# Moving two of a weight pair's four loads from GpSimd's queue to SyncE's

## The chip, the cores and the metric

The kernel runs on one core of a Trainium2 chip. A core has five engines that run side by side and meet through semaphores: PE (TensorE, matrix products), VectorE (DVE in the profile), ScalarE (ACT), GpSimd (POOL) and SyncE (SP). The engines that issue DMAs put them into queues; 16 DMA engines carry the bytes. The metric is the device time of one execution in microseconds. Before the change it was 1569.61 us in the median of 3 runs (1569.16 to 1570.11).

## The reference

Two layers over 512 tokens of width 1024, in fp32. Each layer normalizes x, projects it, runs three token mixers beside each other (windowed attention, a short convolution, a state space model), merges them by gates, and adds the result. Then comes the part that this change touches, the gated feed-forward:

```python
x = x + merged @ w_mix_o[i]
h = rmsnorm(x, norm_ffn[i])
gt, up = jnp.split(h @ w_ffn_in[i], 2, axis=-1)     # 1024 x (2 x 2816)
x = x + (jax.nn.silu(gt) * up) @ w_ffn_out[i]       # 2816 x 1024
```

## The kernel before, in words

Activations lie transposed, channels on the 128 partitions and 512 tokens along them. All weights stream in from DRAM. A product of fp32 matrices is made of three products of parts: a weight tile is split into a rounded high part (a cast on ScalarE) and the remainder (a subtraction on VectorE, line 190, in `lo_of`), and PE multiplies high by high, high by low and low by high (`mm3`, line 270).

The weights are a list of items, in the order of their use. A **plain item** is one load of a tile `raw` (line 185, issued by SyncE), one cast (line 205) and one subtraction. A **pair item** serves most of the feed-forward: of each layer's 22 tiles of hidden channels, tiles 6 to 21 (16 items) and the output products of three groups of tiles (6 items), 22 items a layer and 44 in all. There, two weight matrices and two halves of the operand are multiplied as a 2 x 2 block product with seven products in the place of eight (`seven_products`). For it the weight blocks a11, a12, a21, a22 and four sums of them are wanted. A pair item needs four DMAs from `wsp`, each reading rows of a pre-arranged stretch [a11 a12 | a21 a11 | a22 a21]:

- r2 (line 175, 512 KB) loads a21 and a11; a second DMA (line 176, 512 KB) adds a22 and a21 onto it in flight, so that r2 holds the sums a21 + a22 and a11 + a21;
- r1 (line 177, 512 KB) loads a11 and a12, with nothing added onto it;
- r4 (line 178, 256 KB) loads a22, with nothing added onto it.

From them VectorE makes r3, two further sums of r2 and r1 (lines 216 and 218), ScalarE the high parts h1 to h4 (lines 214, 221, 225, 229), and VectorE the remainders l1 to l4 (line 190). In the profile's groups these names lose their numbers: r1 to r4 are all `r`, h1 to h4 `h`, l1 to l4 `l`.

r1, r2 and r3 come from one pool of five buffers, r4 from a large pool that many temporaries share. A load waits until the earlier user of its buffer is done. Items are fetched two ahead of the one being split, and split until PE has some 48 units of work ready (`feed`).

The sums of the feed-forward's output that go through seven products are added onto `xkept` in DRAM by DMAs with accumulation (lines 1176 and 1179, 256 KB each, issued by GpSimd), eight per group and 24 per layer. `xkept` begins with eight plain stores of the residual (line 1256, SyncE), and it is read back at the end of the layer (line 1233, SyncE). In `seven_products`, ScalarE copies the partial sum pb out (line 1143, `ga`) before PE goes on adding to pb.

Each engine and each issuing queue works in program order, and an instruction that waits holds those behind it. The order on each engine is set when the kernel is built: a scheduler walks the program with modelled times and appends each instruction to its engine's queue. So a load's place in a queue says behind which others it waits.

## Time and profile before

| what | value |
|---|---|
| median of 3 runs | 1569.61 us |
| the profiled execution's own time | 1570.92 us |
| its span, from the first to the last instruction | 1568.9 us |
| PE busy | 1543.0 us (98%) |
| VectorE busy | 1169.3 us (75%) |
| ScalarE busy | 728.8 us (46%) |
| GpSimd busy | 270.5 us (17%) |
| DMA queue 0 (GpSimd's): bytes, share of 16 DMA engines | 100.05 MB, 27.0% |
| DMA queue 1 (SyncE's): bytes, share of 16 DMA engines | 119.60 MB, 23.9% |

Rows of the profile are read so: a time from the span's start, a duration, the engine, the line, the operation, output and input, the count; in brackets how long the engine was idle before it and what ended that idle time. `SPq` is SyncE's queue. A busy PE is not a PE at its peak, since matmuls overlap and their ends are modelled.

### The profile page before, as it was taken

What the parts mean: (1) busy time and instruction counts of PE and PEld (TensorE: products, weight loads), DVE (VectorE), ACT (ScalarE), POOL (GpSimd) and SP (SyncE); (2) the same over time, 40 slices, a digit from 0 to 9 for tenths busy, and PEclk for the clock granted to TensorE, in tenths of its full rate; (3) what the DMA queues carried; (4) which work ended last, traced back from release to release, by engine and by line L of the source; (5) the groups of instructions that cost most, each with busy time, mean ns of one, the idle gap of its engine ahead of it and who ended that gap; (6) DMA issues with size and microseconds to landing.
All of it is one profiled execution on the core that took longest, in us unless ns stands there. A gap on an engine that the chain in (4) does not pass through costs nothing.

```text
span 1568.9 us, 24688 instructions
## 1 busy us (share of the span) xinstructions
PE 1543.0 (98%) x9204; PEld 1350.1 (86%) x9204; DVE 1169.3 (75%) x2292; ACT 728.8 (46%) x1312; POOL 270.5 (17%) x453
## 2 busy tenths in 40 slices
PE   9999999999999999999999999999999999999996
PEld 7777878888888899999888777788888889999996
DVE  7985869765668687978668667897476767878876
ACT  4345543334444365655524554233344434656653
POOL 0301023210000124333021011222100002234221
PEclk9999999999999999999999999999999999999998
DMA  6422334442532679888534232354334237799863
GB/s 225 126 81 79 82 96 131 131 118 79 182 112 95 183 175 221 201 222 195 189 113 130 75 84 87 102 135 131 94 122 167 88 121 197 181 224 212 213 142 118
DMA packets 91959, 221.73 MB, mean 141 GB/s; under 512 B 21600, under 2 KB 27008, under 8 KB 91840
## 3 DMA queue, kind: packets, MB, share of 16 engines
q0 software_dynamic: 36096, 100.05, 27.0%
q1 hardware_dynamic: 55456, 119.60, 23.9%
q8 instruction: 72, 1.18, 0.3%
q10 hardware_dynamic: 288, 0.52, 0.1%
q14 instruction: 47, 0.39, 0.1%
HBM read 193.89 MB, written 22.02 MB: 138 GB/s over the span
## 4 chain that ended last, share of the span: by engine, by line
PE 82%; DVE 6%; DMA 5%; issue 4%; POOL 1%; ACT 1%; DVEq 0%; SPq 0%; POOLq 0%; ACTq 0%
PE pg L270 17%; PE pc L270 11%; PE py L270 8%; PE pd L270 8%; PE pb L270 8%; PE pfo L270 6%; PE px L270 6%; PE pfu L270 4%; PE pfg L270 4%; DMA r<-wsp 3%; PE pu L270 1%; PE pqb L270 1%; PE pz L270 1%; PE pS L852 1%; DVE wlo L190 1%
## 5 line engine op out<-in xcount | busy, mean ns | idle before, releaser
L205 ACT CAST whi<-raw 128x1024 fp32r<-128x1024 f32 (+2 forms) x214 | 195.5, 917 | 431.6 <-PE pg L270 115.3
L190 DVE TENSOR_TENSOR wlo<-raw,whi 128x1024 fp32r<-128x1024 f32 (+2 forms) x214 | 225.9, 1056 | 91.9 <-ACT whi L205 84.1
L190 DVE TENSOR_TENSOR l<-r,h 128x1024 fp32r<-128x1024 f32 (+1 forms) x176 | 187.9, 1086 | 12.1 <-ACT h L225 6.1
L270 PE MATMUL pg<-hi,whi 128*128 128x512 f32 x384 | 152.2, 396 | 0.0
L270 PE MATMUL pg<-hi,wlo 128*128 128x512 f32 x384 | 150.4, 392 | 0.0
L270 PE MATMUL pg<-lo,whi 128*128 128x512 f32 x384 | 150.0, 391 | 0.0
L270 PE MATMUL pd<-lo,h 128*128 128x256 f32 x528 | 148.2, 283 | 0.0
L270 PE MATMUL pd<-hi,l 128*128 128x256 f32 x528 | 147.4, 283 | 0.0
L270 PE MATMUL pd<-hi,h 128*128 128x256 f32 x528 | 147.2, 283 | 0.0
L270 PE MATMUL pb<-hi,h 128*128 128x256 f32 x352 | 100.0, 285 | 3.2 <-ACT ga L1143 2.9
L270 PEld LDWEIGHTS pd<-lo,h 128*128 128x128 f32 x528 | 100.9, 192 | 0.0
L270 PEld LDWEIGHTS pd<-hi,h 128*128 128x128 f32 x528 | 100.5, 192 | 0.0
L270 PEld LDWEIGHTS pd<-hi,l 128*128 128x128 f32 x528 | 100.5, 192 | 0.0
L270 PE MATMUL pb<-lo,h 128*128 128x256 f32 x352 | 99.4, 283 | 0.0
L270 PE MATMUL pb<-hi,l 128*128 128x256 f32 x352 | 98.9, 283 | 0.0
L178 POOL DMA_DIRECT2D r<-wsp x44 | 34.2, 778 | 339.4 <-PE pfu L270 330.6
L270 PEld LDWEIGHTS pg<-hi,whi 128*128 128x128 f32 x384 | 72.1, 188 | 15.8 <-DVE ph_c L354 0.4
L270 PEld LDWEIGHTS pg<-hi,wlo 128*128 128x128 f32 x384 | 72.1, 188 | 15.2
L270 PEld LDWEIGHTS pg<-lo,whi 128*128 128x128 f32 x384 | 72.2, 188 | 14.3
L270 PE MATMUL pc<-hi,whi 128*128 128x512 f32 x192 | 77.3, 402 | 1.7 <-ACT qr L815 1.7
L270 PE MATMUL pc<-lo,whi 128*128 128x512 f32 x192 | 76.0, 396 | 0.0
L270 PE MATMUL pc<-hi,wlo 128*128 128x512 f32 x192 | 75.5, 393 | 0.0
(303 smaller groups left out, 4310.4 us busy)
## 6 DMA issues: line engine op xcount, KB each, us to landing
raw<-wst SPq DMA_DIRECT2D x140, 512.0 KB, 3.5
r<-wsp POOLq DMA_DIRECT2D x132, 512.0 KB, 5.7
raw<-wst SPq DMA_DIRECT2D x56, 256.0 KB, 2.8
r<-wsp POOLq DMA_DIRECT2D x44, 256.0 KB, 5.8
raw<-wst SPq DMA_DIRECT2D x16, 384.0 KB, 3.0
xkept<-ga POOLq DMA_DIRECT2D x24, 256.0 KB, 7.3
xkept<-ub POOLq DMA_DIRECT2D x24, 256.0 KB, 7.7
xkept<-xres SPq DMA_DIRECT2D x16, 256.0 KB, 3.7
```

Source lines behind the costliest of these rows:

```text
L178: nc.gpsimd.dma_start(r4[:, :n], wsp[i, :, 2048 : 2048 + n])
L190: V.tensor_tensor(out=lo, in0=raw, in1=hi.bitcast(F32), op=ALU.subtract)
L205: A.copy(hi[:, c], raw[:, c])
L270: T.matmul(o, a, b, start=start and i == 0, stop=stop and i == 2, skip_group_check=more)
L852: T.matmul(pS[par][:, hp, keys], qt[a][rows, 2 * k + hp], kt[b][rows, k, keys], start=i == 0, stop=i == 2,)
```

## The change

The loads of r1 and r4 are issued by SyncE. r2 and its accumulation stay on GpSimd.

```diff
             n = half[0]
             nc.gpsimd.dma_start(r2[:, : 2 * n], wsp[i, :, 1024 : 1024 + 2 * n])
             nc.gpsimd.dma_start(r2[:, : 2 * n], wsp[i, :, 2048 : 2048 + 2 * n], accum_op=ALU.add)
-            nc.gpsimd.dma_start(r1[:, : 2 * n], wsp[i, :, 0 : 2 * n])
-            nc.gpsimd.dma_start(r4[:, :n], wsp[i, :, 2048 : 2048 + n])
+            nc.sync.dma_start(r1[:, : 2 * n], wsp[i, :, 0 : 2 * n])
+            nc.sync.dma_start(r4[:, :n], wsp[i, :, 2048 : 2048 + n])
             raws.append((i, n, r1, r2, r4))
```

PE, VectorE and ScalarE keep their order. On GpSimd, this is the piece with a group's output sums in layer 0 (the number behind r1, r2, r4, ga and ub is that of the buffer):

```order
 L1176 DMA xkept0_4365<-ga_5848 128x512
 L1179 DMA xkept0_4365<-ub_5849 128x512
 L1176 DMA xkept0_4365<-ga_5929 128x512
 L175 DMA r2_5995<-wsp 128x1024
-L178 DMA r4_6138<-wsp 128x512
 L1179 DMA xkept0_4365<-ub_5930 128x512
-L177 DMA r1_5994<-wsp 128x1024
 L176 DMA r2_5995<-wsp 128x1024
 L1176 DMA xkept0_4365<-ga_5984 128x512
```

The two plain loads between r2 and its accumulation leave; r2 stays behind the three output sums, and the accumulation behind r2.

On SyncE, the first pair item's r1 is placed among the raw loads of the mixers, long before the feed-forward:

```order
 L185 DMA raw_3068<-wst 128x1024
 L185 DMA raw_3089<-wst 128x512
+L177 DMA r1_5020<-wsp 128x1024
 L185 DMA raw_3123<-wst 128x1024
 L185 DMA raw_3150<-wst 128x512
```

A second one (r1_5077) is placed the same way some ten raw loads later, and both again in layer 1.

On SyncE, at the start of the seven-product stretch of layer 0, in the new order:

```order
L185 DMA raw_4961<-wst 128x768
L178 DMA r4_5022<-wsp 128x512
L178 DMA r4_5079<-wsp 128x512
L178 DMA r4_5147<-wsp 128x512
L178 DMA r4_5211<-wsp 128x512
L1256 DMA xkept0_4365<-xres_4068 128x512
L1256 DMA xkept0_4365<-xres_4108 128x512
```

Four r4 loads now stand ahead of the stores to `xkept`. From the last of these stores on, the queue of SyncE holds only r1 and r4 loads up to the next layer's first load (b_c, line 417).

## The prediction

> **What bounds the kernel now.** I read the page first (engine shares, DMA issues), then the windows of the two stretches in which the moved loads are consumed, then who PE and VectorE wait for there, then GpSimd's timeline at one stall.

> ```profile
> span 1568.9 us, 24688 instructions
> PE 1543.0 (98%) x9204; PEld 1350.1 (86%) x9204; DVE 1169.3 (75%) x2292; ACT 728.8 (46%) x1312; POOL 270.5 (17%) x453
> ```

> PE is busy 98% of the span, so a gain can only come out of PE's idle time, and only out of the part that the loads cause. The seven-product stretches run from 536 to 760 us (layer 0) and from 1308 to 1532 us (layer 1):

> ```profile
> core 0: us, PE busy (x) PEld busy (x) DVE busy (x) ACT busy (x) POOL busy (x), PEclk, DMA share, GB/s
> 536.00:760.00 224.00, 221.05 (x1832) 220.18 (x1831) 180.47 (x246) 133.54 (x239) 67.52 (x98) 1.00 0.80 192
> 1308.00:1532.00 224.00, 223.78 (x1861) 223.18 (x1860) 181.22 (x247) 134.72 (x241) 67.60 (x98) 1.00 0.81 194
> 775.00:785.00 10.00, 10.00 (x46) 8.27 (x45) 10.00 (x15) 8.39 (x14) 0.00 (x0) 1.00 0.94 337
> ```

> PE idles 224 - 221.05 = 2.95 us in the first and 0.22 us in the second: together 3.2 us, 0.20% of the time. The granted clock is 1.00 in both. That is the ceiling of any gain here. (The third row gives a price used below: the DMA engines moved 337 GB/s when they were 94% busy.) In layer 0 the idle time has one name:

> ```profile
> PE pb L270 <- ACT ga L1143: 2.9, 2, 1.5
> ```

> Two waits of about 1.5 us, for the copy of pb that frees a partial sum. The copy is late because ScalarE stands behind VectorE, and VectorE behind a load. The one near 692 us:

> ```profile
> 689.66 0.69 DVE L216 TENSOR_TENSOR r<-r,r 128x512 f32<-128x512 f32 x1 [4.33 <-DMA r<-wsp]
> 691.71 0.63 ACT L1164 ACTIVATE ga<-ga 128x512 f32<-128x512 f32 x1 [4.08 <-DVE ga L358]
> 693.18 0.36 ACT L1143 COPY ga<-pb 128x256 f32<-128x256 f32 x1
> ```

> L216 adds r1 to the accumulated r2, so it is r2's accumulation that arrives last. VectorE's waits for that load, first in layer 0's stretch, then in layer 1's:

> ```profile
> DVE r L216 <- DMA r<-wsp: 14.7, 3, 5.6
> DVE r L216 <- DMA r<-wsp: 13.6, 5, 4.9
> ```

> VectorE loses 28.3 us in eight such waits, and PE loses 2.9 us in two: the operands made ahead cover the rest. Layer 1 runs the same program and shows no PE wait, so this cover is just about used up, not plentiful.

> **The change, part by part.** Of an item's four issues, GpSimd keeps r2 (L175) and its accumulation (L176), and loses r1 (L177) and r4 (L178): 44 each, 88 in all.

> *GpSimd's own time.* A quiet item and a crowded one, in the timeline of GpSimd:

> ```profile
> 547.59 0.53 POOL L175 DMA_DIRECT2D r<-wsp  x1 [6.12 <-DVE l L190]
> 549.32 0.53 POOL L177 DMA_DIRECT2D r<-wsp  x1 [1.20 <-DVE l L190]
> 549.84 0.54 POOL L178 DMA_DIRECT2D r<-wsp  x1
> 552.84 0.88 POOL L176 DMA_DIRECT2D r<-wsp  x1 [2.46 <-DMA r<-wsp]
> ...
> 670.36 0.86 POOL L176 DMA_DIRECT2D r<-wsp  x1 [5.31 <-DMA r<-wsp]
> 670.91 1.21 POOL L1176 DMA_DIRECT2D xkept<-ga  x1
> 671.47 1.53 POOL L1179 DMA_DIRECT2D xkept<-ub  x1
> 672.01 1.87 POOL L1176 DMA_DIRECT2D xkept<-ga  x1
> 672.56 1.89 POOL L175 DMA_DIRECT2D r<-wsp  x1
> 673.10 1.90 POOL L178 DMA_DIRECT2D r<-wsp  x1
> 673.65 2.24 POOL L1179 DMA_DIRECT2D xkept<-ub  x1
> 674.22 2.22 POOL L177 DMA_DIRECT2D r<-wsp  x1
> 683.89 0.86 POOL L176 DMA_DIRECT2D r<-wsp  x1 [7.45 <-DMA r<-wsp]
> ```

> An issue holds GpSimd some 0.54 us (549.84 - 549.32 in the quiet item, 673.10 - 672.56 in the crowded one), so 88 x 0.54 = 48 us leave GpSimd. None of it is on the path: in both items r1 and r4 are issued while L176 could not go anyway, because it waits for r2's landing (2.46 us after the last issue in the quiet item, 7.45 us in the crowded one). And in the crowded item r2 itself stands behind the three xkept accumulations, not behind r1 or r4. So L175 and L176 are issued when they are now: 0 us.

> *SyncE's time.* An issue took SyncE 0.33 us (the b_c row below), so 88 x 0.33 = 29 us are added, in stretches where its queue is empty: between 537.5 us, the end of the xkept stores, and b_c at 741.65 us it issues nothing in layer 0. What matters is whether one of these issues waits with weight loads behind it. Rows of SyncE's queue and of GpSimd at the places where the new issues stand among older ones:

> ```profile
> 274.68 7.23 SPq L185 DMA_DIRECT2D raw<-wst  x3
> 275.62 0.57 POOL L177 DMA_DIRECT2D r<-wsp  x1 [13.74 <-DVE apt L358]
> 503.14 1.63 POOL L178 DMA_DIRECT2D r<-wsp  x3 [165.31 <-PE pfu L270]
> 508.09 0.54 POOL L178 DMA_DIRECT2D r<-wsp  x1 [3.32 <-DVE ub L358]
> 516.06 0.33 SPq L1256 DMA_DIRECT2D xkept<-xres  x1
> 524.48 0.54 POOL L175 DMA_DIRECT2D r<-wsp  x1 [15.86 <-DVE l L190]
> 524.90 12.56 SPq L1256 DMA_DIRECT2D xkept<-xres  x4
> 741.65 0.33 SPq L417 DMA_DIRECT2D b_c<-ssb  x1
> ```

> The first r1 stands behind the raw load of 274.68 us; its buffer is free at 275.62 us, under 1 us later, and two more raw loads follow up to 281.9 us. The four r4 loads stand ahead of the store of 516.06 us; the last is free to go at 508.09 us, 8 us before. The 165 us for which GpSimd waited at L178 held nothing back that layer 0 needed: the next r2 went out only at 524.48 us, when VectorE had freed its buffer. I cost the queue on SyncE at 0; if a buffer came later than now, the raw loads behind it would be late by that much.

> *The transfers.* Bytes, shapes and buffers stay. What a load of this kind takes from issue to landing on either queue, on the page:

> ```profile
> raw<-wst SPq DMA_DIRECT2D x140, 512.0 KB, 3.5
> r<-wsp POOLq DMA_DIRECT2D x132, 512.0 KB, 5.7
> raw<-wst SPq DMA_DIRECT2D x56, 256.0 KB, 2.8
> r<-wsp POOLq DMA_DIRECT2D x44, 256.0 KB, 5.8
> ```

> So r1 and r4 may land 2 to 3 us sooner, though these rows mix quiet and crowded stretches. That buys nothing where VectorE waits: there r2's accumulation is last. The question is what r1 and r4 do to r2. Today they follow it in one queue; from SyncE they go beside it, in the crowded items also beside the xkept traffic ahead of it. Bounds on the shift of r2's accumulated landing: if all 512 + 256 KB come in between, 512/337 + 256/337 = 1.5 + 0.8 = +2.3 us. If they are done before, the accumulation no longer finds the rest of r1 on the engines. The rows of L176, its issues and its landing:

> ```profile
> L176 POOL DMA_DIRECT2D r<-wsp x44: 859/878/944, 245.8 to 1502.2; - x44
> DMA to landing us min/median/max: 5.4/5.8/7.7
> ```

> At the stall it took 689.66 - 683.89 = 5.8 us, so at best -0.4 us. Between -0.4 and +2.3 I take +0.4 us, the distance from minimum to median, which is what ordinary sharing costs this transfer today. At the two places without cover that is 2 x 0.4 = +0.8 us on PE; at the other six waits I let the cover swallow it (without cover: 6 x 0.4 = 2.4 us more).

> [...]

> **Sum.** 0 (GpSimd) + 0 (SyncE) + 0.8 (r2 a little later) = +0.8 us on the profiled execution, 1570.92 us, of which 1568.9 us is span. That execution is 1.3 us above the median of the runs, 1569.61 us; on the median the forecast is 1570.4 us. A measurement of this kernel can tell a change from none beyond about 0.2%, 3.1 us: the forecast is no change.

> **Rivals.**

> A. The bursts relax. r1 and r4 out of GpSimd's queue, r2's accumulation comes early enough at both places, and PE's waits go. For it: VectorE's long waits all lie at the xkept bursts, where the queue is fullest. Against it: each burst keeps xkept, r2 and the accumulation, in this order. It needs the accumulation 1.5 us earlier, and the row of L176 allows 0.4. At most all the idle time goes: 1569.6 - 3.2 = 1566.4 us. Chance 0.15.

> B. r2 arrives late, the slower side. r1 goes ahead of or between r2's packets at each burst. For it: 0.80 of the DMA engines' time is taken in the stretch, and r1's wait for its buffer (1.20 us after r2 in the quiet item) puts its issue right into r2's transfer. Against it: total bytes are the same, and part of r1 now goes out while GpSimd still waits. With r1 alone in between, 1.5 us: 2 x 1.5 = 3.0 us at the two stalls, and at the other six, where cover may take half, 6 x 0.75 = 4.5 us: +3.0 to +7.5, 1572.6 to 1577.1 us, middle 1575. It decides from a shift of 0.8 us on (1.6 + 6 x 0.4 = 4.0, or 1.6 with full cover). Chance 0.20. [...]

> C. SyncE's queue is held by an r1 or r4 whose buffer is late, and weight loads stand behind it. The rows above leave about 8 us at 508 us and little at 275 us, with loads made ahead behind it. Losing as much as one wait of the kind of 165 us is excluded, since the same order of issues is kept around it; some 3 us: 1573 us. Chance 0.04.

> **How the numbers follow.** Forecast 0.61, A 0.15, B 0.20, C 0.04. Time 1570.4 us. The range reaches down to A's floor, 1566.4, and up to the middle of B, 1574.8, which leaves out half of B and a little of A, some 0.15. Faster by over 0.2%: A and a trace of the forecast, 0.15, since the ceiling is just that bound; slower: B, C and the forecast's upper edge, 0.26; no change 0.59.

> **What would show it.** GpSimd's busy time falls from 270.5 us by some 50 to 80 us (its issues in a burst last up to 2.2 us). The landing of L177 and L178 falls toward 3 to 4 us. L175 and L176 stay on their places in the bursts; if L176's wait for r2, 7.45 us, grows by 1 us or more, B is at work; if VectorE's eight waits for L216 shrink below 20 us together, A is. PE's idle time in the two windows stays between 2 and 5 us. A gap in SyncE's raw loads after 275 us, or at the same place of layer 1, with PE idle behind it would be C. A gain of more than 3.2 us would prove the ceiling, and so the whole argument, wrong.

## The result, and the profile after

The change made the kernel slower: 1578.86 us in the median of 5 runs (1574.48 to 1583.44), beside 1569.16 us for the kernel before on the same chip. The ratio is 1.0062, with a 95% interval of 1.0045 to 1.0079, or +9.7 us. That lies above the forecast of no change, above the range's end at 1574.8 us, and above all that rival B had been given.

The profiled execution took 1583.44 us, the longest of the five. Its page: span, busy times, and the issues of the moved and the kept loads (count, size, median us from issue to landing).

```profile
span 1581.7 us, 24679 instructions
PE 1548.8 (98%) x9204; PEld 1355.2 (86%) x9204; DVE 1169.9 (74%) x2292; ACT 729.9 (46%) x1312; POOL 222.6 (14%) x365
...
r<-wsp POOLq DMA_DIRECT2D x88, 512.0 KB, 5.8
r<-wsp SPq DMA_DIRECT2D x44, 512.0 KB, 5.1
...
r<-wsp SPq DMA_DIRECT2D x44, 256.0 KB, 5.2
```

GpSimd lost 270.5 - 222.6 = 47.9 us of busy time, just the 48 us of its 88 issues. Nothing came of it. The span is 12.8 us longer. The same windows as before, and the two stretches behind PE's waits in which the granted clock was lower:

```profile
536.00:760.00 224.00, 219.45 (x1801) 218.81 (x1800) 178.49 (x244) 131.42 (x234) 47.57 (x62) 0.98 0.79 190
696.68:703.51 6.83, 5.80 (x27) 5.80 (x28) 6.83 (x13) 4.19 (x9) 1.33 (x2) 0.50 0.96 268
1308.00:1532.00 224.00, 218.87 (x1787) 217.37 (x1786) 177.58 (x243) 130.11 (x232) 48.30 (x63) 0.99 0.81 189
1474.92:1478.33 3.41, 3.41 (x18) 3.41 (x18) 3.41 (x7) 2.02 (x5) 0.00 (x0) 0.50 1.02 287
```

PE idles 4.55 + 5.13 = 9.7 us in the two stretches, where it had idled 3.2 us: 6.5 us more. New is the granted clock, the figure behind the busy times: 0.50 over 6.83 us and over 3.41 us, where it had been 1.00 in the pair stretches. Under the lower clock PE starts a matmul every 0.21 us, in the rest of the pair stretches every 0.12 us. Over the same matmuls of the two stretches PE is busy for 2.28 + 1.56 = 3.8 us longer than before. Together 10.3 of the 12.8 us; about 1 us more is there already at the first pair load (its issue starts at 242.2 us, before at 241.2 us). The five runs lost different amounts of clock: the mean granted clock over the whole run is 0.992 in the profiled one, 0.995 at the median and 0.997 in the fastest (1574.48 us), which is still 5.3 us slower than before. This suggests that the idle time is the steady part of the loss and the clock the varying one; only one of the five runs has a profile to show it.

PE's waits, and VectorE's, in the new profile (sum, times, longest):

```profile
PE pb L270 <- ACT ga L1143: 9.7, 4, 3.1
```

```profile
DVE r L216 <- issue: 41.7, 10, 7.8
```

Both are the chain of the prediction, longer. The profile now puts VectorE's waits down to "issue", but the load is the same one: in the landings of the trace's single DMAs, the accumulation (L176) lands 0.1 us before L216 starts at each of the ten long waits of the pair stretches, and r1 had landed 3 to 10 us earlier. In the profile of before, too, two waits for this load stand under "issue" and are missing from the prediction's eight. They come one item ahead of the bursts of output sums in layer 0:

```profile
615.51 0.69 DVE L216 TENSOR_TENSOR r<-r,r 128x512 f32<-128x512 f32 x1 [1.50 <-issue]
...
678.11 0.69 DVE L216 TENSOR_TENSOR r<-r,r 128x512 f32<-128x512 f32 x1 [3.29 <-issue]
```

So the sum is 33.1 us in ten waits before and 41.7 us in ten after. The largest five waits, in VectorE's timeline, before:

```profile
627.53 0.69 DVE L216 TENSOR_TENSOR r<-r,r 128x512 f32<-128x512 f32 x1 [4.79 <-DMA r<-wsp]
...
739.79 0.69 DVE L216 TENSOR_TENSOR r<-r,r 128x512 f32<-128x512 f32 x1 [5.62 <-DMA r<-wsp]
...
1399.41 0.69 DVE L216 TENSOR_TENSOR r<-r,r 128x512 f32<-128x512 f32 x1 [4.92 <-DMA r<-wsp]
...
1460.08 0.69 DVE L216 TENSOR_TENSOR r<-r,r 128x512 f32<-128x512 f32 x1 [4.78 <-DMA r<-wsp]
```

and the same five places after (the one shown in the prediction, 4.33 us at 689.66, is now the one at 693.77):

```profile
629.94 0.69 DVE L216 TENSOR_TENSOR r<-r,r 128x512 f32<-128x512 f32 x1 [5.88 <-issue]
...
693.77 0.69 DVE L216 TENSOR_TENSOR r<-r,r 128x512 f32<-128x512 f32 x1 [7.33 <-issue]
...
744.26 0.69 DVE L216 TENSOR_TENSOR r<-r,r 128x512 f32<-128x512 f32 x1 [3.44 <-issue]
...
1407.30 0.69 DVE L216 TENSOR_TENSOR r<-r,r 128x512 f32<-128x512 f32 x1 [7.76 <-issue]
...
1470.22 0.69 DVE L216 TENSOR_TENSOR r<-r,r 128x512 f32<-128x512 f32 x1 [7.02 <-issue]
```

Set beside PE's waits for pb behind them, with the wait for the item ahead of each burst (single rows of the timelines, in us; the last row is the sixth long wait of the new profile):

| place | VectorE's wait before | after | the item ahead, before | after | PE's wait before | after |
|---|---|---|---|---|---|---|
| layer 0, first burst of output sums | 4.79 | 5.88 | 1.50 | 1.81 | none | 1.45 |
| layer 0, second burst | 4.33 | 7.33 | 3.29 | 2.01 | 1.39 | 3.10 |
| layer 0, end | 5.62 | 3.44 | | | 1.51 | none |
| layer 1, first burst | 4.92 | 7.76 | 1.36 | 1.01 | none | 2.92 |
| layer 1, second burst | 4.78 | 7.02 | 1.21 | 1.33 | none | 2.18 |
| layer 1, end | 1.34 | 4.14 | | | none | none |

The first five waits grew by 1.09 + 3.00 - 2.18 + 2.84 + 2.24 = 7.0 us, PE's by 6.75 us: in the sum, nearly every microsecond that the load was later reached PE. How much of a wait is covered, that is, does not reach PE, can be worked out from these rows. In layer 1 it is 7.76 - 2.92 = 4.84 and 7.02 - 2.18 = 4.84 us. In layer 0 the item ahead had waited for longer, and what it waited beyond 1.40 us comes on top: 5.88 - 4.84 + (1.81 - 1.40) = 1.45 and 7.33 - 4.84 + (2.01 - 1.40) = 3.10 us, as measured. The same two figures give the wait of before at the second burst, 4.33 - 4.84 + (3.29 - 1.40) = 1.38 us against 1.39 measured, and PE's waits at the bursts of four runs below (r4 alone, r1 alone, r2 alone and all three on SyncE) to 0.02 us. So the three waits of 4.78 to 4.92 us that had cost PE nothing had used their cover up to within 0.1 us. At a layer's end, 5.62 - 1.51 = 4.11 us is covered.

Why the accumulation is later shows at the second burst of layer 0. GpSimd's timeline after:

```profile
672.30 0.87 POOL L176 DMA_DIRECT2D r<-wsp  x1 [6.00 <-DMA r<-wsp]
...
674.47 1.91 POOL L175 DMA_DIRECT2D r<-wsp  x1
675.24 2.01 POOL L1179 DMA_DIRECT2D xkept<-ub  x1
686.70 0.88 POOL L176 DMA_DIRECT2D r<-wsp  x1 [9.45 <-DMA r<-wsp]
```

and the views of the single loads r2 (L175) and r1 (L177) of this item, issue and landing, before:

```profile
L175 POOL DMA_DIRECT2D r<-wsp x1: 1885/1885/1885, 672.6 to 672.6; - x1
...
DMA to landing us min/median/max: 10.8/10.8/10.8
...
L177 POOL DMA_DIRECT2D r<-wsp x1: 2224/2224/2224, 674.2 to 674.2; - x1
...
DMA to landing us min/median/max: 12.3/12.3/12.3
```

and after:

```profile
L175 POOL DMA_DIRECT2D r<-wsp x1: 1911/1911/1911, 674.5 to 674.5; - x1
...
DMA to landing us min/median/max: 11.9/11.9/11.9
...
L177 SPq DMA_DIRECT2D r<-wsp x1: 328/328/328, 676.1 to 676.1; - x1
...
DMA to landing us min/median/max: 8.7/8.7/8.7
```

Before, r1 goes out 1.7 us after r2 and lands after it: 674.2 + 12.3 = 686.5 against 672.6 + 10.8 = 683.4 us. After, r1 still goes out 1.6 us after r2, but lands ahead of it: 676.1 + 8.7 = 684.8 against 674.5 + 11.9 = 686.4 us. From SyncE's queue r1 overtakes r2, and r2 takes 1.1 us longer. In the trace's landings it is so at all four bursts: r1, which landed 3.1 to 3.2 us after r2, now lands 1.6 to 3.8 us ahead of it, r2 takes 0.4 to 1.7 us longer, and r2 and its accumulation together take 16.3 to 18.9 us, before 16.0 to 16.5 us. The next item's r1 then goes out at 684.1 us, ahead of its own r2 (687.25 us), while this item's accumulation still has to run, and the accumulation takes 7.0 us instead of 5.7 us.

### The profile page after: what moved, and what is told of

Read it like the earlier page. It is cut to its first block, busy times and chain, and to the rows that moved or that the text cites. A ratio compares the mean times of both kernels' runs of the same rounds, so it can differ in the third digit from the quotient of the medians.

```text
span 1581.7 us, 24679 instructions
## 1 busy us (share of the span) xinstructions
PE 1548.8 (98%) x9204; PEld 1355.2 (86%) x9204; DVE 1169.9 (74%) x2292; ACT 729.9 (46%) x1312; POOL 222.6 (14%) x365
## 4 chain that ended last, share of the span: by engine, by line
PE 85%; issue 6%; DMA 3%; DVE 2%; POOL 2%; ACT 1%; SPq 0%; DVEq 0%; POOLq 0%; ACTq 0%
PE pg L270 17%; PE pc L270 11%; PE py L270 8%; PE pd L270 8%; PE pb L270 8%; PE pfo L270 6%; PE px L270 6%; PE pfu L270 4%; PE pfg L270 4%; PE pu L270 3%; PE pqb L270 2%; DMA r<-wsp 2%; PE pz L270 1%; PE pS L852 1%; PE po L898 1%
## 5 line engine op out<-in xcount | busy, mean ns | idle before, releaser
L190 DVE TENSOR_TENSOR wlo<-raw,whi 128x1024 fp32r<-128x1024 f32 (+2 forms) x214 | 225.8, 1056 | 89.6 <-ACT whi L205 82.5
L190 DVE TENSOR_TENSOR l<-r,h 128x1024 fp32r<-128x1024 f32 (+1 forms) x176 | 187.9, 1085 | 11.6 <-ACT h L214 4.0
L270 PE MATMUL pg<-hi,whi 128*128 128x512 f32 x384 | 152.2, 396 | 0.0
L270 PE MATMUL pg<-hi,wlo 128*128 128x512 f32 x384 | 150.4, 392 | 0.0
L270 PE MATMUL pg<-lo,whi 128*128 128x512 f32 x384 | 150.0, 391 | 0.0
L270 PE MATMUL pd<-lo,h 128*128 128x256 f32 x528 | 148.3, 283 | 0.0
L270 PE MATMUL pd<-hi,l 128*128 128x256 f32 x528 | 147.5, 283 | 0.0
L270 PE MATMUL pd<-hi,h 128*128 128x256 f32 x528 | 147.3, 283 | 0.0
L270 PE MATMUL pb<-hi,h 128*128 128x256 f32 x352 | 100.8, 287 | 9.7 <-ACT ga L1143 9.7
L175 POOL DMA_DIRECT2D r<-wsp x44 | 31.1, 706 | 547.7 <-DVE l L190 461.5
L270 PEld LDWEIGHTS pd<-lo,h 128*128 128x128 f32 x528 | 101.1, 192 | 0.0
L270 PEld LDWEIGHTS pd<-hi,h 128*128 128x128 f32 x528 | 100.7, 192 | 0.0
L270 PEld LDWEIGHTS pd<-hi,l 128*128 128x128 f32 x528 | 100.6, 192 | 0.0
L270 PE MATMUL pb<-lo,h 128*128 128x256 f32 x352 | 100.2, 285 | 0.0
L270 PE MATMUL pb<-hi,l 128*128 128x256 f32 x352 | 99.8, 285 | 0.0
L270 PEld LDWEIGHTS pg<-hi,whi 128*128 128x128 f32 x384 | 72.1, 188 | 15.8 <-DVE at_nm L352 0.4
L270 PEld LDWEIGHTS pg<-hi,wlo 128*128 128x128 f32 x384 | 72.1, 188 | 15.2
L270 PEld LDWEIGHTS pg<-lo,whi 128*128 128x128 f32 x384 | 72.2, 188 | 14.3
L270 PE MATMUL pc<-hi,whi 128*128 128x512 f32 x192 | 78.0, 406 | 2.4 <-ACT qr L815 2.4
L270 PEld LDWEIGHTS pb<-hi,h 128*128 128x128 f32 x352 | 68.3, 194 | 10.7 <-ACT ga L1143 10.7
L270 PE MATMUL pc<-lo,whi 128*128 128x512 f32 x192 | 76.5, 398 | 0.0
## 6 DMA issues: line engine op xcount, KB each, us to landing
raw<-wst SPq DMA_DIRECT2D x140, 512.0 KB, 3.5
r<-wsp POOLq DMA_DIRECT2D x88, 512.0 KB, 5.8
r<-wsp SPq DMA_DIRECT2D x44, 512.0 KB, 5.1
raw<-wst SPq DMA_DIRECT2D x56, 256.0 KB, 2.8
r<-wsp SPq DMA_DIRECT2D x44, 256.0 KB, 5.2
xkept<-ga POOLq DMA_DIRECT2D x24, 256.0 KB, 6.7
xkept<-ub POOLq DMA_DIRECT2D x24, 256.0 KB, 9.1
```

The lines of the kernel that those rows point to most:

```text
L175: nc.gpsimd.dma_start(r2[:, : 2 * n], wsp[i, :, 1024 : 1024 + 2 * n])
L190: V.tensor_tensor(out=lo, in0=raw, in1=hi.bitcast(F32), op=ALU.subtract)
L270: T.matmul(o, a, b, start=start and i == 0, stop=stop and i == 2, skip_group_check=more)
```

## The experiments

The expectations use these letters. **S**: the loads on the second queue share the DMA engines with r2 and its accumulation while these are in flight; r2 is late, and each late item makes the next one late, since its r2 waits for one of the five buffers. **Q**: SyncE's queue is held by a load whose buffer is late. **P**: it is not the sharing; something about loads on two queues as such. Each time is compared with the kernel before on the same chip, whose median was 1568.1 to 1569.5 us.

### Each moved load alone

Diffs are against the change where nothing else is said. r4 alone on SyncE:

```diff
-            nc.sync.dma_start(r1[:, : 2 * n], wsp[i, :, 0 : 2 * n])
+            nc.gpsimd.dma_start(r1[:, : 2 * n], wsp[i, :, 0 : 2 * n])
             nc.sync.dma_start(r4[:, :n], wsp[i, :, 2048 : 2048 + n])
```

> Only r4 (256 KB, line 178) goes to SyncE, r1 stays on GpSimd. Theory S (sharing): a plain load on the second queue takes the DMA engines from r2 while r2 is in flight, in proportion to its bytes; r4 is a third of the bytes moved by the change, so about a third of its loss of 9.7 us, some +1 to +4 us (1570 to 1573), and the median landing of r2 (4.8 us before, 5.5 us in the change) near 5.0. Theory Q (a queue on SyncE blocks: an r4 that waits for its buffer holds r1 and others behind it): r4 is the one that waits longest, but with no r1 behind it nothing is held, so 0 (1569).

Measured: 1571.46 us, ratio 1.0018 (1.0006 to 1.0029), +3.3 us.

r1 alone on SyncE:

```diff
             nc.sync.dma_start(r1[:, : 2 * n], wsp[i, :, 0 : 2 * n])
-            nc.sync.dma_start(r4[:, :n], wsp[i, :, 2048 : 2048 + n])
+            nc.gpsimd.dma_start(r4[:, :n], wsp[i, :, 2048 : 2048 + n])
```

> Only r1 (512 KB, line 177) goes to SyncE, r4 stays on GpSimd. Theory S: two thirds of the bytes, and r1's buffer comes free 1.7 us after r2's issue, right in r2's transfer: +5 to +9 us (1574 to 1578), r2's median landing 5.2 to 5.5 us. Theory Q: with no r4 ahead of it r1 is never held on SyncE: 0 (1569).

Measured: 1574.16 us, ratio 1.0040 (1.0024 to 1.0057), +6.0 us. The two add up to 9.3 us of the change's 9.7 us. They are in the order of their bytes, 256 and 512 KB, but with intervals of 0.9 to 4.5 and 3.8 to 8.9 us more can't be said of their proportion. PE's waits and one window with a lower clock, of r4 alone:

```profile
PE pb L270 <- ACT ga L1143: 4.2, 4, 2.4
```

```profile
634.00:638.00 4.00, 3.52 (x18) 3.52 (x19) 4.00 (x6) 3.37 (x8) 1.07 (x2) 0.57 0.94 244
```

and of r1 alone:

```profile
PE pb L270 <- ACT ga L1143: 4.6, 3, 2.5
```

```profile
1467.00:1472.00 5.00, 4.88 (x28) 4.88 (x29) 5.00 (x9) 3.12 (x8) 0.17 (x1) 0.66 0.99 270
```

Each load has its own waits for pb (1.3 and 1.7 us more than before) and one stretch of 3.41 us at half the clock (some 1.4 and 1.5 us of PE's time, an estimate from the matmuls in these windows, x18 and x28, at 0.12 us each), 2.7 and 3.2 us in all; with r1 alone some 2.8 us of the median's +6.0 us are not accounted for by this one profile. With r4 alone on SyncE, r1 stays behind r2 in one queue, and r2 with its accumulation takes no longer at the bursts than before (15.8 to 16.6 us). What is late there is r2 of the item ahead: 8.4, 7.4 and 8.0 us at three of the four bursts, before 7.1, 6.9 and 6.7 us. So the overtaking by r1 is not the whole of the loss.

Q expected nothing from either run, since each has only one of the two loads on SyncE. It needs a held queue; in the change's own queue of SyncE the raw loads behind the first r1 go out as before, the whole program being 1 us later by then:

```profile
271.27 4.74 SPq L185 DMA_DIRECT2D raw<-wst  x2
276.35 0.33 SPq L177 DMA_DIRECT2D r<-wsp  x1
...
279.57 3.34 SPq L185 DMA_DIRECT2D raw<-wst  x2
```

So Q falls.

### The opposite: r2 moved, r1 and r4 left

Against the kernel before:

```diff
-            nc.gpsimd.dma_start(r2[:, : 2 * n], wsp[i, :, 1024 : 1024 + 2 * n])
+            nc.sync.dma_start(r2[:, : 2 * n], wsp[i, :, 1024 : 1024 + 2 * n])
```

r1, r4 and the accumulation stay on GpSimd.

> The other way round: the first load of r2 (line 175) goes to SyncE, r1, r4 and the accumulations stay on GpSimd. Theory S: r2 no longer stands behind the three output accumulations in GpSimd's queue, it only shares the engines with them, so the wait of the accumulation for r2 at the bursts falls from 7 to 11 us toward 5 us, VectorE's waits for line 216 fall from 28 us to under 15, PE's two waits (2.9 us) go: 1566 to 1568.5 us. If a second queue costs as such, whichever load is on it: 1574 or more.

Measured: 1568.00 us, ratio 0.9996 (0.9987 to 1.0006): no change. Two queues are used here too, with 512 KB per item on SyncE as in the run with r1 alone, which lost 6.0 us. The urgent load is now the one on the second queue. So a second queue does not cost as such (P would have been 1574 us or more). In the trace's landings r2 takes 5.04 us in the mean and 8.8 us at the longest, where it took 5.50 and 10.8 us before and 6.00 and 12.5 us in the change, while r1's median goes up to 6.2 us. PE's waits for pb are all but gone from this profile:

```profile
PE pb L270 <- ACT ga L1143: 0.3, 1, 0.3
```

VectorE's waits for L216 are 24.6 us, not under 15 as expected. The profiled execution was 1565.45 us, which fits 2.6 us less waiting, but the medians are equal. What a smaller wait can bring here is no more than the runs' own spread.

### All three plain loads on SyncE

```diff
-            nc.gpsimd.dma_start(r2[:, : 2 * n], wsp[i, :, 1024 : 1024 + 2 * n])
+            nc.sync.dma_start(r2[:, : 2 * n], wsp[i, :, 1024 : 1024 + 2 * n])
             nc.gpsimd.dma_start(r2[:, : 2 * n], wsp[i, :, 2048 : 2048 + 2 * n], accum_op=ALU.add)
             nc.sync.dma_start(r1[:, : 2 * n], wsp[i, :, 0 : 2 * n])
             nc.sync.dma_start(r4[:, :n], wsp[i, :, 2048 : 2048 + n])
```

> All three plain loads (r2, r1, r4) on SyncE, only accumulations on GpSimd. Theory S: r2 is ahead of r1 and r4 in one queue, as before, and no longer behind the output accumulations: 1566 to 1568.5 us, as with r2 alone. If what costs is that r1 and r4 left GpSimd: 1575 to 1580, as in the change.

Measured: 1571.33 us, ratio 1.0018 (1.0003 to 1.0032), +3.2 us: a miss. r2 was as early as hoped (5.10 us in the mean), but the accumulation, the other half of what L216 waits for, came late in places:

```profile
L176 POOL DMA_DIRECT2D r<-wsp x44: 835/854/951, 247.7 to 1510.2; - x44
...
DMA to landing us min/median/max: 5.2/5.9/12.5
```

Its longest landing is 12.5 us, before 7.7 us. It is the sum of r2 and accumulation at the bursts that must not be late. There it is 17.4 to 19.1 us in this run, 16.0 to 16.5 us before and 16.0 to 16.8 us with r2 alone on SyncE, while the mean over all items (11.6 us, before 11.7 us) shows nothing. That r1 and r4 take the engines from the accumulation here is the likely reason; no run separates it. The profile is of an execution of 1577.44 us, 6 us above the median.

### One queue, but r1 and r4 ahead

```diff
+            nc.gpsimd.dma_start(r1[:, : 2 * n], wsp[i, :, 0 : 2 * n])
+            nc.gpsimd.dma_start(r4[:, :n], wsp[i, :, 2048 : 2048 + n])
             nc.gpsimd.dma_start(r2[:, : 2 * n], wsp[i, :, 1024 : 1024 + 2 * n])
             nc.gpsimd.dma_start(r2[:, : 2 * n], wsp[i, :, 2048 : 2048 + 2 * n], accum_op=ALU.add)
-            nc.sync.dma_start(r1[:, : 2 * n], wsp[i, :, 0 : 2 * n])
-            nc.sync.dma_start(r4[:, :n], wsp[i, :, 2048 : 2048 + n])
```

> All four loads stay on GpSimd, but r1 and r4 are issued ahead of r2 instead of behind it (in this kernel lines 175 and 176 are r1 and r4, 177 and 178 r2 and its accumulation). No second queue is involved. Theory S (what costs is that r2 lands later, whatever is on the engines before it): r2 takes the buffer that comes free 1.7 us later and stands behind 768 KB, some 2.3 us at 337 GB/s, so its accumulation is up to 4 us later per item, more than in the change: +9 us or more (1577 and up). Theory P (two queues running beside each other cost as such, by switching between them): r2 in one queue loses nothing but the order, 0 to +3 us (1568 to 1571).

Measured: 1600.05 us, ratio 1.0189 (1.0172 to 1.0207), +30.6 us. One queue, as in the kernel before, with the same bytes; only the order is turned. PE's waits and the windows:

```profile
PE pb L270 <- ACT ga L1143: 21.0, 8, 4.0
```

```profile
536.00:765.00 229.00, 218.12 (x1758) 217.26 (x1757) 175.04 (x239) 128.35 (x230) 67.46 (x98) 0.96 0.75 185
1308.00:1545.00 237.00, 227.79 (x1783) 224.04 (x1781) 179.30 (x244) 129.81 (x229) 70.21 (x102) 0.97 0.76 190
```

The waits for pb are 18 us longer than before, and 4% and 3% of the two stretches' clock are gone (229 x 0.04 + 237 x 0.03 = 16 us, some of it inside the waits). So a second queue is not needed for the loss (P falls here too); r2 behind 768 KB of less urgent loads is enough. The order also makes r2 wait for the buffers of r1 and r4, and VectorE's order differs at one place in each layer; these are not separated from the bytes ahead. The change lost about a third of this, which would fit an r2 that is overtaken only in part.

### Holding r1 and r4 back

The change, with two one-column writes on GpSimd (into r1 and r4) placed behind the issue of the accumulation, so that the two loads can only go out after it:

```diff
+            acc = nc.gpsimd.dma_start(r2[:, : 2 * n], wsp[i, :, 2048 : 2048 + 2 * n], accum_op=ALU.add)
+            with tc.issue_after(acc.ins): nc.gpsimd.memset(r1[:, 0:1], 0.0), nc.gpsimd.memset(r4[:, 0:1], 0.0)
+            nc.sync.dma_start(r1[:, : 2 * n], wsp[i, :, 0 : 2 * n]), nc.sync.dma_start(r4[:, :n], wsp[i, :, 2048 : 2048 + n])
```

> The change, but r1 and r4 on SyncE are held back until GpSimd has issued r2's accumulation (two one-column memsets on GpSimd behind that issue, which the loads overwrite; this is the added work). r2's first load then has the engines to itself, apart from output accumulations, and the accumulation shares them with r1 and r4. Theory S in its narrow form (harm only while r2's first load is in flight): r2's landing back from 5.5 to 4.8 us in the median, time back to +0 to +3 us (1568 to 1571). Wide form (harm through any sharing in the chain r2, accumulation, r3, and r1 now 5 us later): +6 us or more (1574 and up).

Measured: 1615.20 us, ratio 1.0292 (1.0276 to 1.0307), +45.7 us. PE's longest group of waits is a new one:

```profile
PE pd L270 <- ACT ub L1146: 25.4, 13, 6.1
```

The waits for the copy of pb no longer appear among PE's long ones, but r1 and r4 became the late loads: VectorE now waits 35.2 us for h4, which is made of r4, where it waited 0.5 us before. The added writes also hold GpSimd until r1's and r4's buffers are free (at their line it waits 330.5 us in four waits). By its time this is the wide form's case, but the run changes too much at once, and it leaves open how much of the change's loss is the overtaking at the bursts alone. What it shows is that r1 and r4 have little slack of their own.

### A sixth buffer

By S, lateness adds up since r2 waits for a buffer. With six buffers for r1, r2 and r3, and one fewer in the large pool:

```diff
-    NU2 = 58
-    NHI, NLO, NRAW, NPART = 5, 5, 2, 5
+    NU2 = 57
+    NHI, NLO, NRAW, NPART = 5, 5, 2, 6
```

> The change with six buffers for r1, r2 and r3 instead of five (and 57 instead of 58 buffers in the large pool, to make room). Theory S says that a later r2 costs because the next r2 waits for a buffer that is freed only after the late one is used; with a sixth buffer r2 is asked for earlier, the lateness is covered: 1566 to 1570, the four PE waits of the change gone. If the loss sits on the DMA engines' capacity and not in this loop, the sixth buffer changes nothing: 1575 to 1580.

> The kernel before with six buffers (and 57 in the large pool), the control of the run above. Theory S: VectorE's waits for line 216 fall from 28 us toward 10, PE's two waits go: 1565 to 1568. If the large pool misses its buffer, 1570 or more for both kernels alike.

Measured: the change so 1587.96 us, ratio 1.0117 (1.0100 to 1.0134); the kernel before so 1593.07 us, ratio 1.0151 (1.0134 to 1.0168). Both are slower, as the control's expectation had allowed, for a reason of their own, which this row of PE's waits has in either (here the change's; in the kernel before with five buffers 2.9 us, longest 1.4):

```profile
PE po L898 <- ACT pt L888: 11.3, 2, 5.6
```

The missing buffer of the large pool stalls the attention twice, and the clock falls behind it (in the change so, 0.66 in the mean of the 10 us behind each wait). As a test this was spoiled; only the difference between the two, with the change 5 us ahead, hinted that its loss was gone. So the room was taken elsewhere, from the rotary step's temporaries (one buffer each in place of two), and the large pool kept its 58:

```diff
-    NHI, NLO, NRAW, NPART = 5, 5, 2, 5
+    NHI, NLO, NRAW, NPART = 5, 5, 2, 6
...
-        ta, tb = small([P, nh, HALF], f"ro_a{nh}"), small([P, nh, HALF], f"ro_b{nh}")
-        td, te = small([P, nh, HALF], f"ro_c{nh}"), small([P, nh, HALF], f"ro_d{nh}")
+        ta, tb = (small([P, nh, HALF], f"ro_{i}{nh}", bufs=1) for i in "ab")
+        td, te = (small([P, nh, HALF], f"ro_{i}{nh}", bufs=1) for i in "cd")
```

The kernel before with it:

> The kernel before with six buffers for r1, r2, r3; the room comes from the temporaries of the rotary step (one each instead of two, all used by VectorE alone), so the large pool keeps its 58. Theory S with the loop of buffers: the two waits of PE at 692 and 744 us go, the waits at 232 and 1004 us stay as before (1.4 us each, not 5.6 as with 57 buffers): 1564 to 1567 us. If the sixth buffer itself, by the new order, makes the waits of 5.6 us: 1580 and more.

The change with it:

> The change with the same six buffers. Theory S with the loop: the change's loss is gone, 1564 to 1568 us, within 2 us of the run above. If sharing costs apart from the loop, it stays 5 to 10 us above the run above: 1571 or more.

r2 alone on SyncE with it:

> r2's first load on SyncE, r1 and r4 on GpSimd, with the same six buffers. Theory S: 1563 to 1567 us, not slower than the two above. If the three agree within 1 us, PE is the only bound that is left in this stretch and the queue of a load no longer matters.

Measured: the kernel before so 1574.97 us, ratio 1.0034 (1.0023 to 1.0045); the change so 1570.55 us, 1.0007 (0.9998 to 1.0017); r2 on SyncE so 1568.06 us, 0.9995 (0.9985 to 1.0004). All three lie above what was expected, the first by 8 us and the others by 2.6 and 1.1 us, and they don't agree within 1 us. With six buffers the change's 9.7 us shrink to 1.9 us beside the kernel before with five, which its interval does not tell from none; beside the kernel before with six, moving r1 and r4 is 4.4 us faster. PE's waits and the window of layer 0, of the change with six buffers:

```profile
PE pb L270 <- ACT ga L1143: 1.6, 2, 1.3
```

```profile
536.00:765.00 229.00, 228.99 (x1880) 227.53 (x1879) 183.23 (x251) 136.70 (x242) 47.04 (x61) 1.00 0.77 189
```

PE idles 0.01 us in that stretch and keeps its clock. Yet the loads are no quicker: r2 and its accumulation take 5.94 + 7.17 us in the mean, in the change with five buffers 6.00 + 6.19 us. They are issued earlier before their use: from r2's issue to L216 it is 18.5 us in the median (without the first two items of a layer), with five buffers 15.2 us. So the time from issue to landing did not cost the 9.7 us as such; the likely reading is that it did with no buffer to issue ahead into. The sixth buffer also makes the scheduler order PE, VectorE and ScalarE in another way (the same in all three kernels), which these runs don't separate from the buffer itself. Why the kernel before lost 6.3 us with six buffers stays open: its profile, of an execution of 1572.41 us, shows 2.4 us of waits for pb, less than the 2.9 us with five buffers.

No run was measurably faster than the kernel before.

## Why the prediction was wrong, point by point

**The ceiling was not broken, and half of the argument held.** No edit of the loads' queues won anything that the runs can tell. GpSimd's 48 us of issues were worth 0 us, and SyncE's queue 0 us. Rival C fell with the rows of SyncE's queue; rival A never showed, since VectorE's waits grew from 33.1 us (28.3 us by the prediction's count) to 41.7 us.

**The step that failed is "at the two places without cover that is 2 x 0.4 = +0.8 us on PE; at the other six waits I let the cover swallow it".** It failed in two ways.

First, the size. In the mean of all 44 items the shift was well taken: r2's landing went from 5.50 to 6.00 us and the accumulation's from 6.24 to 6.19 us, together +0.45 us, beside the predicted +0.4. But the shift does not fall evenly. Where VectorE waits, at the bursts of output sums, the wait grew by 1.1 to 3.0 us, as far as the upper bound of +2.3 us and beyond. A typical delay, read as the distance from minimum to median over all items, was applied to the places where r2 takes longest (9.9 to 10.8 us before, 4.8 us in the median). The upper bound, made from the bytes over the 337 GB/s measured with the DMA engines 94% busy, was the better guide for these. Nor were the two named places the ones: at 692 us PE's wait grew by 1.7 us, while the one at the end of layer 0 went away.

Second, the cover. The waits of VectorE of 4.8 to 4.9 us that held nobody up were taken as covered with room to spare, though the prediction itself said of layer 1 that the cover was just about used up. At a burst 4.84 us are covered, so three of the "other six" stood at the edge, and all growth there went to PE. That the wait of 4.33 us had cost PE 1.39 us, and one of 4.92 us nothing, was the sign in the rows of before: the difference lies in the wait of 3.29 us one item earlier, which the prediction's eight rows leave out. Growth of 1.1 to 3.0 us at four places without cover, less the one wait that went away, makes the 6.5 us of PE's idle time.

**A term was missing: the clock.** At two of the four waits the granted clock fell to 0.50, and that cost 3.8 us in the profiled execution. Nothing in the prediction priced a wait at more than its length.

**Rival B was the mechanism, with a chance of 0.20, and priced at 3.0 to 7.5 us.** r1 landing ahead of r2 is what it said, r1 and r4 each lose when moved alone, and the same loads ahead of r2 in one queue lose three times as much. What was held against it, that the total of bytes is the same, has no weight: the run with r2 moved has the same bytes and loses nothing, so it is the order that counts. Missing from its price were the clock and r4, which the prediction left out of B ("with r1 alone in between") and which alone cost 3.3 us. Moving the issues took 47.9 us off GpSimd and still cost 9.7 us, since the one queue had also kept an order: in the profile of before r1 lands 1.3 to 7.1 us after its r2 in every item but the first two of a layer, in the change it lands 1.6 to 6.0 us ahead in eight of these 40.

**The signs.** GpSimd's busy time came as announced (-47.9 us). The landings of L177 and L178 did not: 5.1 and 5.2 us, not 3 to 4. VectorE's waits for L216 did not shrink, and PE's idle time, 9.7 us, left the 2 to 5 us given for it. L176's wait for r2 at the burst grew from 7.45 to 9.45 us, over the 1 us that was to point to B; but the sign was badly made, since about 1.1 us of it is just the two issues that no longer fill the gap. From r2's issue to L176's the growth is 0.9 us (11.3 to 12.2). The better sign was at hand: which of r1 and r2 lands first.

## What to carry to other kernels

As these runs show it, a load's place behind another in one queue is a priority: before you move it to another engine's queue, see which urgent transfer it stands behind, since from a second queue it may overtake that one, as r1 did here by 1.6 to 3.8 us at the bursts. Price the delay where the consumer waits already, with the bytes that can come in between over the measured rate of busy engines (here 337 GB/s), and not with the typical spread over all transfers; and take cover from the waits that do and do not reach the bound engine, since a wait that reaches it nowhere may have no room left. Count a wait together with the one of the item before it, since both draw on the same cover. If the loads must be spread, give the second queue the urgent one; another buffer for it to be issued ahead into may help, but no run here shows that by itself.

## What the runs showed of the hardware that was not expected

```profile
693.27:696.68 3.41, 1.34 (x12) 1.13 (x10) 2.88 (x4) 0.86 (x2) 0.86 (x1) 1.00 0.04 13
1406.66:1410.07 3.41, 1.65 (x14) 1.45 (x13) 2.74 (x4) 0.72 (x2) 0.87 (x1) 1.00 0.31 123
1410.07:1413.48 3.41, 2.25 (x18) 2.25 (x19) 3.41 (x6) 3.41 (x7) 0.56 (x1) 1.00 0.93 149
1471.51:1474.92 3.41, 1.23 (x10) 1.02 (x10) 3.41 (x5) 2.65 (x5) 1.42 (x2) 1.00 0.52 66
```

PE idled 2.07 and 2.18 us in the stretches ahead of a fall, and the wait of 2.92 us was split into 1.76 and 1.16 us. So in this trace it was the place of a wait on the grid, and not its length alone, that went with the loss of clock. How much idle time brings a fall is not shown: at the end of the program the clock fell behind a stretch with 1.64 us (1567.08 to 1570.49 us, by the profile's modelled ends), and behind the 1.76 us it did not.

An accumulation of 512 KB into a buffer on the chip took 5.2 to 5.5 us at the least in every run here, while r2's plain load of the same size took 3.4 to 4.0 us at the least. And r1 was hardly quicker for leaving GpSimd's queue: 5.1 us in the median from GpSimd before, and 5.1 us from SyncE after.
